# The values of a hybrid block's last four attention heads: products of 512 columns in place of 256, each for two token blocks, with the weights loaded once for each half of the tokens

## The chip, the cores and the metric

The kernel runs on one core of one Trainium2 chip. The metric is device time in microseconds (us) of one execution. The core has TensorE (PE, matrix products, with its weight loads PEld), VectorE (DVE), ScalarE (ACT), GpSimd (POOL) and SyncE (SP), whose queue issues nearly all transfers between the chip's main memory and the core. Engines run side by side, each through its own queue in order, and wait for one another by semaphores.

## The reference, cut to what matters

One layer: `x += W_out concat[StickBreakingAttn(6 heads), GatedConv(4 groups), GatedDeltaNet(6 heads)](RMSNorm(x))`, then a squared-ReLU MLP and a final norm; 512 tokens, model width 2048, all in float32. The part at hand is the stick-breaking attention, whose heads are 128 wide:

```python
proj = h @ w_in                      # sb_q, sb_k, sb_v are 768 columns each
z = einsum(q_blk, k) * scale
log_fail = where(causal, -softplus(z), 0.0)
rem = cumsum(log_fail, reverse=True) - log_fail
w = where(causal, exp(log_sigmoid(z) + rem), 0.0)
out = einsum(w, v)
```

The change concerns the columns of `sb_v` that belong to heads 2 to 5.

## The kernel before, in words

Every float32 operand of a large product is split into a high part in TensorE's fast float format and a low remainder; a product is three TensorE products: high by high, high by low, low by high (`mm3`, or the three lines in `v_stage`). The normalised input is kept in on-chip memory as 16 tiles `xw[k]` (128 rows of the model width by 512 tokens, high and low). Weights come through `wload`: a transfer of 128 x 512 numbers (256 KB) into `raw`, a cast on ScalarE into `whi` (L103), and a subtraction on VectorE into `wlo` (L104); each of the three has four buffers, and the function has a raised priority. `gemm` makes one 128 x 512 result in a PSUM bank `mm` (three banks) with four loads and 48 products of 512 columns, 12 to a load.

The kernel has these stages: a first pass over the input, which also makes the values of heads 0 and 1; the delta-net heads with the convolution groups; from about 525 us the stick-breaking heads; from about 740 us the output product (16 `gemm` results, one for each 128 of the model's columns); the MLP's two products.

A stick-breaking head `h` takes two `gemm` results, q and k (`sb_qk`, split by `sb_split` at L575, L576 and copied in part at L578), and the values (`vt[h // 2]`: high and low in `vhl`, the last block in full in `v3`). `sb_attn` is a chain: the products z (three lines of `mm3`, and a small one at L600) into three PSUM banks; scaling into `zs` (L601) and a mask on GpSimd (L604); L606 on VectorE; two steps on ScalarE (L607, L608); L610 and L611 on VectorE; four scans (L615); L617; an exponential on ScalarE (L618); ten transposes on TensorE (L626) into the same three banks; the split into `hl` (L630, L631, L633); ten products with the values into `o` (L639 to L643); and a copy into the head's `y` (L645). The tiles `zs`, `e`, `sp` and `hl` exist once, so one head's chain follows the other's.

The values of heads 2 and 3 are made by `v_stage(1)`, those of 4 and 5 by `v_stage(2)`: eight loads each, one load holding two row tiles of 256 columns, and for each row tile and each of the four token blocks three products of 256 columns, into halves of two `mm` banks. They are then scaled and split by `v_evac` (L230, L231, L234).

The order of instructions on each engine is not written out by hand. A scheduler places them when the kernel is built, by the program's order, priorities and its own estimate of durations; each engine then follows its list. The program's order in this stage before is: q and k of head 0, head 0, q and k of 1, head 1, `v_stage(1)`, q and k of 2, head 2, q and k of 3, head 3, q and k of 4, `v_stage(2)`, head 4, q and k of 5, head 5, and `gdn_gate(5)` (one `gemm`). Then follow the split of the 16 `y` tiles (L726, L727) and the output products; each of these runs through the `y` tiles in the order of `ORDER`, where head 5's is the 15th and head 5 of the delta net's the last.

Of the kernel before, what the change touches and what calls it, by code (L numbers as in the profile page):

```python
# [11 lines left out]
F32 = mybir.dt.float32  # L12
F32R = mybir.dt.float32r
AF = mybir.ActivationFunctionType
ALU = mybir.AluOpType

P = 128
T = 512
NB = T // P
D = 2048  # L20
KT = D // P
# [33 lines left out]
def trunk(ctx, tc, xT, wv1, wv2, wa, wo, wu, wd, vec, wf, out, dbg=None):  # L55
    nc = tc.nc
    V, S, G, PE = nc.vector, nc.scalar, nc.gpsimd, nc.tensor
# [39 lines left out]
    def wload(src, n, prio=None):  # L97
        with tc.high_priority(WPRIO if prio is None else prio):
            raw = per.tile([P, 512], F32, name="raw", tag="raw", bufs=4)
            nc.sync.dma_start(out=raw[:, :n], in_=src)  # L100
            hi = per.tile([P, 512], F32R, name="whi", tag="whi", bufs=4, align_bytes=256)
            lo = per.tile([P, 512], F32R, name="wlo", tag="wlo", bufs=4, align_bytes=256)
            S.copy(out=hi[:, :n], in_=raw[:, :n])  # L103
            V.tensor_tensor(out=lo[:, :n], in0=raw[:, :n], in1=hi[:, :n].bitcast(F32), op=ALU.subtract)  # L104
        return hi, lo
# [73 lines left out]
    xw = []  # L179
# [7 lines left out]
    for k in range(KT):  # L187
        hi, lo = wload(wv1[:, k, :], 268, 0)
# [6 lines left out]
                               op0=ALU.mult, op1=ALU.subtract)  # L195
        for b in range(NB):
            s = slice(b * P, (b + 1) * P)
# [15 lines left out]
    p = xps("r")  # L213
    PE.matmul(p, lhsT=ones, rhs=acc, start=True, stop=True)
    rsqrt_exp(R, p, 1.0 / D, None)
    rtok = pt([P, NB], "rtok")
    p = xps("r")
# [3 lines left out]
    rtoks = pt([P, NB], "rtoks")  # L221
    S.mul(out=rtoks, in_=rtok, mul=SCALE)

    def v_evac(src_of_blk, pool):

        hl = pool.tile([P, 2, NB, 256], F32R, name="vhl", bufs=2)
        v3 = pool.tile([P, 256], F32, name="v3", bufs=2)
        for b in range(NB):
            src = src_of_blk(b)
            S.activation(out=hl[:, 0, b], in_=src, func=AF.Copy, scale=rtok[:, b:b + 1])  # L230
            V.scalar_tensor_tensor(out=hl[:, 1, b], in0=src, scalar=rtok[:, b:b + 1],  # L231
                                   in1=hl[:, 0, b].bitcast(F32), op0=ALU.mult, op1=ALU.subtract)
            if b == NB - 1:
                S.activation(out=v3, in_=src, func=AF.Copy, scale=rtok[:, b:b + 1])  # L234
        return hl, v3

    vt = [None] * 3
    ab = pt([P, NB, 12], "ab")
# [8 lines left out]
        nc.sync.dma_start(out=vd[:, 2 * c:2 * c + 2].rearrange("p b f -> p (b f)"), in_=t)  # L247

    def v_load():
        hl = sp_pool.tile([P, 2, NB, 256], F32R, name="vhl", bufs=2)  # L250
        v3 = sp_pool.tile([P, 256], F32, name="v3", bufs=2)
        for c in range(2):
            t = tmp()
            nc.sync.dma_start(out=t, in_=vd[:, 2 * c:2 * c + 2].rearrange("p b f -> p (b f)"))
            o = hl[:, :, 2 * c:2 * c + 2].rearrange("p w b f -> p w (b f)")
            S.copy(out=o[:, 0], in_=t)
            V.tensor_tensor(out=o[:, 1], in0=t, in1=o[:, 0].bitcast(F32), op=ALU.subtract)
            if c == 1:
                S.copy(out=v3, in_=t[:, 256:512])
        vt[0] = (hl, v3)  # L260

    def v_stage(i):
        pp = [mmps(), mmps()]
        for c in range(0, KT, 2):
            hi, lo = wload(wv2[i - 1][:, c:c + 2, :].rearrange("p k f -> p (k f)"), 512)
            for kk in range(2):
                k = c + kk
                ws = slice(kk * 256, kk * 256 + 256)
                for b in range(NB):
                    s = slice(b * P, (b + 1) * P)  # L270
                    o = pp[b // 2][:, (b % 2) * 256:(b % 2) * 256 + 256]
                    PE.matmul(o, lhsT=xw[k][:, 0, s], rhs=hi[:, ws], start=k == 0 and b % 2 == 0, stop=False)  # L272
                    PE.matmul(o, lhsT=xw[k][:, 0, s], rhs=lo[:, ws], start=False, stop=False)  # L273
                    PE.matmul(o, lhsT=xw[k][:, 1, s], rhs=hi[:, ws], start=False, stop=k == KT - 1 and b % 2 == 1)  # L274
        vt[i] = v_evac(lambda b: pp[b // 2][:, (b % 2) * 256:(b % 2) * 256 + 256], sp_pool)

    ys = [None] * KT

# [294 lines left out]
    def sb_split(p, name):  # L573
        hl = sp_pool.tile([P, 2, 512], F32R, name=name, tag=name, bufs=2)
        S.copy(out=hl[:, 0], in_=p)  # L575
        V.tensor_tensor(out=hl[:, 1], in0=p, in1=hl[:, 0].bitcast(F32), op=ALU.subtract)  # L576
        l0 = sp_pool.tile([P, P], F32, name=name + "0", tag=name + "0", bufs=2)
        S.copy(out=l0, in_=p[:, 0:P])  # L578
        return hl, l0

# [2 lines left out]
    def sb_qk(h):  # L583
        qk[h] = sb_split(gemm(wa[24 + 2 * h], xw), "sq") + sb_split(gemm(wa[24 + 2 * h + 1], xw), "sk")
# [107 lines left out]
    v_load()  # L692
    sb_attn(0)
    sb_qk(1)
    sb_attn(1)
    v_stage(1)
    sb_qk(2)
    sb_attn(2)
    sb_qk(3)
    sb_attn(3)  # L700
    sb_qk(4)
    v_stage(2)
    sb_attn(4)
    sb_qk(5)
    sb_attn(5)
# [426 lines left out]
def layout(x, norm1_w, w_in, sc_conv_w, gdn_conv_w, gdn_a_log, gdn_dt_bias, gdn_norm_w,  # L1132
           w_out, norm2_w, w_up, w_down, final_norm_w):
    win = w_in[0]
    kc = lambda a: np.ascontiguousarray(a)
    cols = []
    for h in range(NH):
        cols += [3840 + 768 + h * P, 3840 + h * P, 3840 + 1536 + h * P]
    cols += [6144 + h * P for h in range(NH)]
    for h in range(NH):  # L1140
        cols += [h * P, 768 + h * P]
    for g in range(NG):
        cols += [2816 + g * P, 3328 + g * P, 2304 + g * P]
    wt = _ktile(win)
    wa = kc(np.stack([wt[:, :, c:c + P] for c in cols]))
    wv1 = kc(np.concatenate([wt[:, :, 1536:1792], wt[:, :, 6912:6924]], axis=2))
    wv2 = kc(np.stack([wt[:, :, 1792:2048], wt[:, :, 2048:2304]]))
    wo = _ktile(w_out[0]).reshape(P, KT, KT, P)[:, ORDER]
    wo = kc(wo.transpose(2, 0, 1, 3))


    wu = _ktile(w_up[0]).reshape(P, KT // 2, 2, FF // P // 2, 2, P)
    wu = kc(wu.transpose(3, 2, 4, 0, 1, 5).reshape(FF // P // 2, 2, 2, P, KT // 2 * P))


    wd = _ktile(w_down[0]).reshape(P, FF // P // (2 * HK), HK, 2, 2, 2, 512)
    wd = kc(wd.transpose(1, 5, 3, 4, 0, 2, 6).reshape(FF // P // (2 * HK), 2, 2, 2, P, HK * 512))
    wf = kc(np.broadcast_to(final_norm_w[None, :], (P, D)))
    pcol = lambda v: v.reshape(-1, P).T
    rep = lambda v: np.broadcast_to(v[None, :], (P, v.shape[0]))  # L1160
    scw = sc_conv_w[0].reshape(3, NG, P).transpose(2, 1, 0).reshape(P, 12)
    gcw = gdn_conv_w[0].reshape(4, 18, P).transpose(2, 1, 0).reshape(P, 72)
    vec = kc(np.concatenate([
        pcol(norm1_w[0]), pcol(norm2_w[0]), scw, gcw,
        rep(gdn_a_log[0]), rep(gdn_dt_bias[0]), gdn_norm_w[0].reshape(P, 1)], axis=1))
    xT = kc(_ktile(x[0].T))
    return dict(xT=xT, wv1=wv1, wv2=wv2, wa=wa, wo=wo, wu=wu, wd=wd, vec=vec, wf=wf)
# [14 lines left out]
```

## Time and profile before

| what | value |
|---|---|
| median of 3 runs | 2176.17 us (2174.32 to 2177.16) |
| the profiled execution, its own time | 2174.82 us |
| its span, first to last instruction | 2173.1 us |
| TensorE busy | 2143.5 us, 99% |
| VectorE, ScalarE, GpSimd busy | 77%, 49%, 6% |
| stick-breaking stage | about 525 to 740 us |

The span is what the views of the trace divide up; 1.7 us of the execution's own time lie around it. An engine's busy time counts an instruction from its start to its end; since TensorE's products overlap in a pipeline, the distance between their starts, not their duration, says how many fit into a time.

### The profile page before, as it was taken

Reading aid. Unit: us, or ns where it says so; the run is one execution under the profiler, and the core shown is the slowest. Engines: PE = TensorE matmul, PEld = TensorE weight load, DVE = VectorE, ACT = ScalarE, POOL = GpSimd, SP = SyncE. Lnnn points to the kernel's source line nnn. Section 1 sums busy time; section 2 is a strip of 40 time slices with the busy share of each in tenths; the row PEclk is TensorE's granted clock in tenths of the full one; section 3 lists DMA queues with packets and bytes.
Section 4 is the critical chain, followed back from the end, with each engine's and each line's share of the span. In section 5 each row is a group of like instructions: output and inputs, shape, how many; then the busy total and the mean of one; then the engine's idle time right before and its main releaser. Section 6 shows DMA issues by size and latency. Waiting matters only on the chain.

```text
span 2173.1 us, 33090 instructions
## 1 busy us (share of the span) xinstructions
PE 2143.5 (99%) x12674; PEld 1885.9 (87%) x12674; DVE 1663.8 (77%) x2348; ACT 1070.9 (49%) x1622; POOL 140.0 (6%) x191
## 2 busy tenths in 40 slices
PE   9999999999999999999999999999999999999997
PEld 8887888888988888799999999999788888888886
DVE  6688977644667655688788878887898898899887
ACT  5646665333435544454545444544444454445454
POOL 0000000000000011000000000000001010000102
PEclk9999999999999999999999999999999999999998
DMA  5333232322222344666666666656987777787764
GB/s 188 103 103 96 80 89 91 92 95 83 83 83 83 112 155 141 218 180 172 201 195 179 171 202 196 178 172 201 310 263 185 232 223 219 192 236 212 185 196 116
DMA packets 158974, 353.80 MB, mean 163 GB/s; under 512 B 20192, under 2 KB 61152, under 8 KB 158688
## 3 DMA queue, kind: packets, MB, share of 16 engines
q1 hardware_dynamic: 144704, 300.83, 40.9%
q0 software_dynamic: 13824, 50.34, 13.6%
q8 instruction: 99, 1.62, 0.3%
q14 instruction: 59, 0.48, 0.1%
q10 hardware_dynamic: 288, 0.52, 0.1%
HBM read 307.33 MB, written 44.31 MB: 162 GB/s over the span
## 4 chain that ended last, share of the span: by engine, by line
PE 94%; DMA 2%; DVE 2%; ACT 1%; issue 1%; SPq 0%; ACTq 0%; DVEq 0%
PE mm L110 11%; PE mm L109 11%; PE mm L111 11%; PE pu L109 10%; PE pu L111 10%; PE pu L110 10%; PE pp L110 9%; PE pp L109 9%; PE pp L111 9%; PE mm L273 1%; PE mm L274 1%; PE mm L272 1%; DMA xq<-xs 1%; DMA tmp<-x 1%; PE i L397 1%
## 5 line engine op out<-in xcount | busy, mean ns | idle before, releaser
L828 ACT CAST W<-q 128x1024 fp32r<-128x1024 f32 x446 | 465.4, 1051 | 573.7 <-PE pp L111 260.1
L829 DVE TENSOR_TENSOR W<-q,W 128x1024 fp32r<-128x1024 f32 x446 | 542.1, 1223 | 128.8 <-ACT W L828 124.5
L109 PE MATMUL mm<-big,whi 128*128 128x512 f32 x1024 | 404.6, 395 | 1.4 <-ACT whi L103 0.8
L110 PE MATMUL mm<-big,whi 128*128 128x512 f32 x1024 | 403.8, 394 | 0.0
L111 PE MATMUL mm<-big,wlo 128*128 128x512 f32 x1024 | 402.4, 393 | 0.0
L109 PE MATMUL pp<-W,A 128*128 128x512 f32 x896 | 348.3, 391 | 7.9 <-DVE xq L993 5.3
L110 PE MATMUL pp<-W,A 128*128 128x512 f32 x896 | 350.3, 391 | 2.1 <-DVE W L829 2.1
L111 PE MATMUL pp<-W,A 128*128 128x512 f32 x896 | 349.7, 390 | 1.1 <-DVE A L829 1.1
L104 DVE TENSOR_TENSOR wlo<-raw,whi 128x512 fp32r<-128x512 f32 (+1 forms) x292 | 196.3, 674 | 158.5 <-ACT whi L103 150.6
L103 ACT CAST whi<-raw 128x512 fp32r<-128x512 f32 (+1 forms) x292 | 176.9, 607 | 276.7 <-PE mm L110 238.7
L109 PE MATMUL pu<-XS,W 128*128 128x256 f32 x1024 | 288.4, 282 | 1.1 <-ACT W L828 0.6
L111 PE MATMUL pu<-XS,W 128*128 128x256 f32 x1024 | 287.7, 281 | 0.8 <-DVE W L829 0.8
L110 PE MATMUL pu<-XS,W 128*128 128x256 f32 x1024 | 288.0, 281 | 0.0
L109 PEld LDWEIGHTS mm<-big,whi 128*128 128x128 f32 x1024 | 192.4, 188 | 40.9 <-ACT whi L103 1.2
L110 PEld LDWEIGHTS mm<-big,whi 128*128 128x128 f32 x1024 | 192.5, 188 | 39.1 <-DVE big L727 0.3
L111 PEld LDWEIGHTS mm<-big,wlo 128*128 128x128 f32 x1024 | 192.4, 188 | 38.8
L109 PEld LDWEIGHTS pp<-W,A 128*128 128x128 f32 x896 | 169.1, 189 | 45.1 <-DVE xq L993 5.7
L110 PEld LDWEIGHTS pp<-W,A 128*128 128x128 f32 x896 | 169.1, 189 | 38.3 <-DVE W L829 3.3
L111 PEld LDWEIGHTS pp<-W,A 128*128 128x128 f32 x896 | 168.9, 189 | 36.6 <-DVE A L829 1.5
L846 DVE TENSOR_TENSOR q<-q 128x1024 f32<-128x1024 f32 x160 | 195.8, 1224 | 2.3 <-DMA q<-in_wu_dram 0.9
L109 PEld LDWEIGHTS pu<-XS,W 128*128 128x128 f32 x1024 | 194.1, 190 | 2.3 <-ACT W L828 1.5
L111 PEld LDWEIGHTS pu<-XS,W 128*128 128x128 f32 x1024 | 194.0, 190 | 1.0 <-DVE W L829 1.0
(290 smaller groups left out, 3269.1 us busy)
## 6 DMA issues: line engine op xcount, KB each, us to landing
q<-in_wu_dram SPq DMA_DIRECT2D x128, 512.0 KB, 4.5
q<-in_wd_dram SPq DMA_DIRECT2D x128, 512.0 KB, 5.5
raw<-in_wa_dram SPq DMA_DIRECT2D x192, 256.0 KB, 2.9
hs<-h SPq DMA_DIRECT2D x32, 1024.0 KB, 5.6
q<-in_wd_dram POOLq DMA_DIRECT2D x64, 512.0 KB, 7.5
ha<-hs SPq DMA_DIRECT2D x55, 512.0 KB, 6.4
raw<-in_wo_dram SPq DMA_DIRECT2D x64, 256.0 KB, 2.9
q<-in_wu_dram POOLq DMA_DIRECT2D x32, 512.0 KB, 5.5
```

What stands on the lines that cost most here:

```text
L103: S.copy(out=hi[:, :n], in_=raw[:, :n])
L104: V.tensor_tensor(out=lo[:, :n], in0=raw[:, :n], in1=hi[:, :n].bitcast(F32), op=ALU.subtract)
L109: PE.matmul(p, lhsT=lh, rhs=rh, start=first, stop=False, skip_group_check=more)
L110: PE.matmul(p, lhsT=lh, rhs=rl, start=False, stop=False, skip_group_check=more)
L111: PE.matmul(p, lhsT=ll, rhs=rh, start=False, stop=last, skip_group_check=more)
L272: PE.matmul(o, lhsT=xw[k][:, 0, s], rhs=hi[:, ws], start=k == 0 and b % 2 == 0, stop=False)
L273: PE.matmul(o, lhsT=xw[k][:, 0, s], rhs=lo[:, ws], start=False, stop=False)
L274: PE.matmul(o, lhsT=xw[k][:, 1, s], rhs=hi[:, ws], start=False, stop=k == KT - 1 and b % 2 == 1)
L397: PE.matmul(pv[:, b], lhsT=kq[:, 2 * c + b, 0], rhs=kq[:, 2 * c + b], start=True, stop=True)
L828: S.copy(out=o[:, 0], in_=src)
L829: V.tensor_tensor(out=o[:, 1], in0=src, in1=o[:, 0].bitcast(F32), op=ALU.subtract)
L846: on_v = lambda t, u: V.tensor_tensor(out=t, in0=t, in1=u, op=ALU.add)
```

## The change

`v_stage` goes, and `v_half` comes. Each load now holds one row tile of all 512 columns (heads 2 to 5), and `v_half(0)` multiplies it with token blocks 0 and 1, `v_half(1)` with blocks 2 and 3; the four heads' values of half the tokens come out of 16 loads and 96 products of 512 columns. The program has `v_half(0)` ahead of head 1 and `v_half(1)` ahead of head 2, since each half is needed from head 2 on. A third buffer for `vhl` holds all values at once, and the small copies `sq0` and `sk0` lose one of their two buffers. The weights' layout in memory is changed to match. Lines behind the edit move up by three to five: L626 becomes L623, L639 to L643 become L636 to L640, L100 to L111 stay.

```diff
--- before.py
+++ after.py
@@ -221,18 +221,13 @@
     rtoks = pt([P, NB], "rtoks")
     S.mul(out=rtoks, in_=rtok, mul=SCALE)
 
-    def v_evac(src_of_blk, pool):
-
-        hl = pool.tile([P, 2, NB, 256], F32R, name="vhl", bufs=2)
-        v3 = pool.tile([P, 256], F32, name="v3", bufs=2)
-        for b in range(NB):
-            src = src_of_blk(b)
-            S.activation(out=hl[:, 0, b], in_=src, func=AF.Copy, scale=rtok[:, b:b + 1])
-            V.scalar_tensor_tensor(out=hl[:, 1, b], in0=src, scalar=rtok[:, b:b + 1],
-                                   in1=hl[:, 0, b].bitcast(F32), op0=ALU.mult, op1=ALU.subtract)
-            if b == NB - 1:
-                S.activation(out=v3, in_=src, func=AF.Copy, scale=rtok[:, b:b + 1])
-        return hl, v3
+    def v_block(b, src, hl, v3):
+
+        S.activation(out=hl[:, 0, b], in_=src, func=AF.Copy, scale=rtok[:, b:b + 1])
+        V.scalar_tensor_tensor(out=hl[:, 1, b], in0=src, scalar=rtok[:, b:b + 1],
+                               in1=hl[:, 0, b].bitcast(F32), op0=ALU.mult, op1=ALU.subtract)
+        if b == NB - 1:
+            S.activation(out=v3, in_=src, func=AF.Copy, scale=rtok[:, b:b + 1])
 
     vt = [None] * 3
     ab = pt([P, NB, 12], "ab")
@@ -247,7 +242,7 @@
         nc.sync.dma_start(out=vd[:, 2 * c:2 * c + 2].rearrange("p b f -> p (b f)"), in_=t)
 
     def v_load():
-        hl = sp_pool.tile([P, 2, NB, 256], F32R, name="vhl", bufs=2)
+        hl = sp_pool.tile([P, 2, NB, 256], F32R, name="vhl", bufs=3)
         v3 = sp_pool.tile([P, 256], F32, name="v3", bufs=2)
         for c in range(2):
             t = tmp()
@@ -259,20 +254,22 @@
                 S.copy(out=v3, in_=t[:, 256:512])
         vt[0] = (hl, v3)
 
-    def v_stage(i):
+    def v_half(half):
+
         pp = [mmps(), mmps()]
-        for c in range(0, KT, 2):
-            hi, lo = wload(wv2[i - 1][:, c:c + 2, :].rearrange("p k f -> p (k f)"), 512)
-            for kk in range(2):
-                k = c + kk
-                ws = slice(kk * 256, kk * 256 + 256)
-                for b in range(NB):
-                    s = slice(b * P, (b + 1) * P)
-                    o = pp[b // 2][:, (b % 2) * 256:(b % 2) * 256 + 256]
-                    PE.matmul(o, lhsT=xw[k][:, 0, s], rhs=hi[:, ws], start=k == 0 and b % 2 == 0, stop=False)
-                    PE.matmul(o, lhsT=xw[k][:, 0, s], rhs=lo[:, ws], start=False, stop=False)
-                    PE.matmul(o, lhsT=xw[k][:, 1, s], rhs=hi[:, ws], start=False, stop=k == KT - 1 and b % 2 == 1)
-        vt[i] = v_evac(lambda b: pp[b // 2][:, (b % 2) * 256:(b % 2) * 256 + 256], sp_pool)
+        for k in range(KT):
+            hi, lo = wload(wv2[:, k], 512)
+            for i in range(2):
+                b = 2 * half + i
+                s = slice(b * P, (b + 1) * P)
+                mm3(pp[i], xw[k][:, 0, s], xw[k][:, 1, s], hi, lo, k == 0, k == KT - 1)
+        for i in range(2):
+            if half == 0:
+                vt[1 + i] = (sp_pool.tile([P, 2, NB, 256], F32R, name="vhl", bufs=3), None)
+            else:
+                vt[1 + i] = (vt[1 + i][0], sp_pool.tile([P, 256], F32, name="v3", bufs=2))
+            for j in range(2):
+                v_block(2 * half + j, pp[j][:, i * 256:i * 256 + 256], *vt[1 + i])
 
     ys = [None] * KT
 
@@ -574,7 +571,7 @@
         hl = sp_pool.tile([P, 2, 512], F32R, name=name, tag=name, bufs=2)
         S.copy(out=hl[:, 0], in_=p)
         V.tensor_tensor(out=hl[:, 1], in0=p, in1=hl[:, 0].bitcast(F32), op=ALU.subtract)
-        l0 = sp_pool.tile([P, P], F32, name=name + "0", tag=name + "0", bufs=2)
+        l0 = sp_pool.tile([P, P], F32, name=name + "0", tag=name + "0", bufs=1)
         S.copy(out=l0, in_=p[:, 0:P])
         return hl, l0
 
@@ -692,14 +689,14 @@
     v_load()
     sb_attn(0)
     sb_qk(1)
+    v_half(0)
     sb_attn(1)
-    v_stage(1)
     sb_qk(2)
+    v_half(1)
     sb_attn(2)
     sb_qk(3)
     sb_attn(3)
     sb_qk(4)
-    v_stage(2)
     sb_attn(4)
     sb_qk(5)
     sb_attn(5)
@@ -1144,7 +1141,7 @@
     wt = _ktile(win)
     wa = kc(np.stack([wt[:, :, c:c + P] for c in cols]))
     wv1 = kc(np.concatenate([wt[:, :, 1536:1792], wt[:, :, 6912:6924]], axis=2))
-    wv2 = kc(np.stack([wt[:, :, 1792:2048], wt[:, :, 2048:2304]]))
+    wv2 = kc(wt[:, :, 1792:2304])
     wo = _ktile(w_out[0]).reshape(P, KT, KT, P)[:, ORDER]
     wo = kc(wo.transpose(2, 0, 1, 3))
```

SP's queue, from the end of the delta-net stage to the first output weights; `raw` of `in_wv_dram` is a value load, of `in_wa_dram` one for `gemm`, of `in_wo_dram` one for the output product. Before:

```order
L254 DMA tmp<-vd 128x512 x2
L100 DMA raw<-in_wa_dram 128x512 x16
L100 DMA raw<-in_wv_dram 128x512 x8
L100 DMA raw<-in_wa_dram 128x512 x24
L100 DMA raw<-in_wv_dram 128x512 x8
L100 DMA raw<-in_wa_dram 128x512 x12
L100 DMA raw<-in_wo_dram 128x512 x17
```

and with the change:

```order
L249 DMA tmp<-vd 128x512 x2
L100 DMA raw<-in_wa_dram 128x512 x16
L100 DMA raw<-in_wv_dram 128x512 x16
L100 DMA raw<-in_wa_dram 128x512 x8
L100 DMA raw<-in_wv_dram 128x512 x16
L100 DMA raw<-in_wa_dram 128x512 x28
L100 DMA raw<-in_wo_dram 128x512 x17
```

The value loads are 32 in place of 16; 28 loads of q, k and gate weights stand behind the last of them, where 12 stood.

TensorE around head 5's transposes (`z<-ident,zs`); `o` is the product with the values, `mm<-big` here the output product. Before:

```order
L111 MATMUL mm<-big,wlo 128x512
L626 MATMUL z<-ident,zs 128x128 x10
L109 MATMUL mm<-big,whi 128x512
L110 MATMUL mm<-big,whi 128x512
L111 MATMUL mm<-big,wlo 128x512
...
L110 MATMUL mm<-big,whi 128x512
L639 MATMUL o<-hl,vhl 128x512
L111 MATMUL mm<-big,wlo 128x512
L109 MATMUL mm<-big,whi 128x512
...
L640 MATMUL o<-hl,vhl 128x512
L641 MATMUL o<-hl,vhl 128x512
```

and with the change, from the last product ahead of the transposes to the first behind the head:

```order
L111 MATMUL mm<-big,wlo 128x512
L623 MATMUL z<-ident,zs 128x128 x10
L636 MATMUL o<-hl,vhl 128x512
L637 MATMUL o<-hl,vhl 128x512
L638 MATMUL o<-hl,vhl 128x512
L636 MATMUL o<-hl,vhl 128x384
...
L638 MATMUL o<-hl,vhl 128x256
L640 MATMUL o<-w_6941,v_6189 128x128
L109 MATMUL mm<-big,whi 128x512 x3
L110 MATMUL mm<-big,whi 128x512
```

Output products stood between the transposes and the products `o`, and between the first and the second of these; now the ten follow the transposes directly. Ahead of the transposes, back to head 5's last z product, stand 81 products of 512 columns before, and 54 now.

VectorE in head 5's chain, from the step on the masked `zs` (L606 before, L603 now) to the split of the transposed weights (`hl`). Before:

```order
L606 SCALAR_TENSOR_TENSOR e<-zs 128x1280
L135 TENSOR_TENSOR tmp<-tmp 128x512
L104 TENSOR_TENSOR wlo<-raw,whi 128x512
L548 TENSOR_TENSOR y<-y,tmp 128x512
L610 SCALAR_TENSOR_TENSOR sp<-zs,e 128x1280
L104 TENSOR_TENSOR wlo<-raw,whi 128x512
L611 SCALAR_TENSOR_TENSOR zs<-zs,e 128x1280
L104 TENSOR_TENSOR wlo<-raw,whi 128x512
...
L615 SCALAR_TENSOR_TENSOR e<-ones,sp 128x255
L617 TENSOR_TENSOR zs<-zs,e 128x1280
L104 TENSOR_TENSOR wlo<-raw,whi 128x512 x3
L631 TENSOR_TENSOR hl<-z,hl 128x512 x2
```

and with the change:

```order
L603 SCALAR_TENSOR_TENSOR e<-zs 128x1280
L607 SCALAR_TENSOR_TENSOR sp<-zs,e 128x1280
L104 TENSOR_TENSOR wlo<-raw,whi 128x512
L608 SCALAR_TENSOR_TENSOR zs<-zs,e 128x1280
L104 TENSOR_TENSOR wlo<-raw,whi 128x512
...
L612 SCALAR_TENSOR_TENSOR e<-ones,sp 128x255
L104 TENSOR_TENSOR wlo<-raw,whi 128x512
L614 TENSOR_TENSOR zs<-zs,e 128x1280
L628 TENSOR_TENSOR hl<-z,hl 128x512 x2
L628 TENSOR_TENSOR hl<-z,hl 128x256
```

The gate's two steps (on `tmp` and `y`) stand ahead of it now, and the chain's own steps are the same ones.

## Rows read from the trace of the kernel before

**Rows 1.** The page: its head, TensorE's busy time (part 1), the chain (part 4).

```profile
span 2173.1 us, 33090 instructions
...
PE 2143.5 (99%) x12674; PEld 1885.9 (87%) x12674; DVE 1663.8 (77%) x2348; ACT 1070.9 (49%) x1622; POOL 140.0 (6%) x191
...
PE 94%; DMA 2%; DVE 2%; ACT 1%; issue 1%; SPq 0%; ACTq 0%; DVEq 0%
```

**Rows 2.** Windows, 525 to 740 us: length, then each engine's busy us (instructions).

```profile
525.00:740.00 215.00, 214.24 (x1191) 187.33 (x1190) 138.18 (x195) 99.11 (x171) 8.91 (x24) 1.00 0.26 81
```

**Rows 3.** Timeline of TensorE, 563 to 585 us: start, us, engine, line, operation.

```profile
564.02 0.28 PE L274 MATMUL mm<-whi,big 128*128 128x256 f32 x1
...
568.70 0.28 PE L274 MATMUL mm<-whi,big 128*128 128x256 f32 x1
...
569.98 0.39 PE L111 MATMUL mm<-big,wlo 128*128 128x512 f32 x1
...
584.94 0.39 PE L111 MATMUL mm<-big,wlo 128*128 128x512 f32 x1
```

**Rows 4.** Lines by shape, TensorE, 525 to 740 us: busy us, mean ns.

```profile
L273 PE MATMUL mm<-wlo,big 128*128 128x256 f32 x128 | 36.4, 285 | 0.0
```

**Rows 5.** Lines and DMA issues, 525 to 740 us: the loads' work.

```profile
L104 DVE TENSOR_TENSOR wlo<-raw,whi 128x512 fp32r<-128x512 f32 x65 | 44.7, 688 | 44.5 <-ACT whi L103 42.2 <-PE z L626 1.8
...
L103 ACT CAST whi<-raw 128x512 fp32r<-128x512 f32 x66 | 40.8, 619 | 69.6 <-PE mm L110 48.2 <-PE mm L274 17.0 <-issue 3.3
...
raw<-in_wv_dram SPq DMA_DIRECT2D x14, 256.0 KB, 2.7
```

**Rows 6.** Timeline of TensorE, 711 to 739 us, around head 5's steps.

```profile
712.19 0.39 PE L600 MATMUL z<-sk,sq 128*128 128x128 f32 x2
...
730.79 1.25 PE L626 MATMUL z<-ident,zs 128*128 128x128 f32 x10
...
731.80 0.48 PE L109 MATMUL mm<-big,whi 128*128 128x512 f32 x1
...
738.53 0.39 PE L643 MATMUL o<-w,v 128*128 128x128 f32 x2
```

**Rows 7.** Timeline of VectorE, 712 to 734 us, head 5's chain.

```profile
712.74 0.35 DVE L601 SCALAR_TENSOR_TENSOR zs<-z,rtoks,R 128x128 f32<-128x128 f32 x1
...
718.02 1.49 DVE L610 SCALAR_TENSOR_TENSOR sp<-zs,e 128x1280 f32<-128x1280 f32 x1 [0.85 <-ACT e L608]
...
719.42 0.68 DVE L104 TENSOR_TENSOR wlo<-raw,whi 128x512 fp32r<-128x512 f32 x1
...
722.50 2.96 DVE L615 TENSOR_TENSOR_SCAN e<-ones,sp 128x511 f32<-128x511 f32 x4
...
725.49 1.49 DVE L617 TENSOR_TENSOR zs<-zs,e 128x1280 f32<-128x1280 f32 x1
...
732.05 1.62 DVE L631 TENSOR_TENSOR hl<-z,hl 128x512 fp32r<-128x512 f32 x3
```

**Rows 8.** Timeline of ScalarE, 715 to 741 us, head 5's chain.

```profile
715.40 1.28 ACT L607 ACTIVATE e<-e 128x1280 f32<-128x1280 f32 x1 [0.34 <-DVE e L606]
...
727.08 1.27 ACT L618 ACTIVATE zs<-zs 128x1280 f32<-128x1280 f32 x1 [2.50 <-DVE zs L617]
...
738.95 0.59 ACT L645 COPY y<-o 128x512 f32<-128x512 f32 x1 [3.68 <-PE o L643]
...
739.95 1.14 ACT L726 CAST big<-y 128x512 fp32r<-128x512 f32 x2
```

**Rows 9.** Timeline: two waits; windows after the second, PEclk third from right.

```profile
1559.10 0.50 PE L110 MATMUL pp<-W,A 128*128 128x512 f32 x1 [1.41 <-DVE W L829]
...
1566.69 0.50 PE L109 MATMUL pp<-W,A 128*128 128x512 f32 x1 [2.08 <-ACT A L828]
...
1567.20:1570.40 3.20, 3.13 (x8) 2.19 (x8) 2.94 (x3) 1.43 (x2) 0.00 (x0) 0.50 1.03 251
...
1570.60:1573.80 3.20, 3.20 (x15) 2.63 (x15) 0.85 (x2) 1.05 (x1) 0.00 (x0) 1.00 1.08 398
```

## Prediction

> **What bounds the kernel now.** I read the page first. TensorE is busy in 99% of the span and the chain that ended last is 94% TensorE [rows 1], so what shortens or delays TensorE's own stream is what counts. The change lies in the stick-breaking stage, so the second view is the window 525 to 740 us, where TensorE is busy for 214.24 of 215 us, VectorE for 138.18 and ScalarE for 99.11, at a granted clock of 1.00 [rows 2]. TensorE has no wait there to be taken away. Two things can move the time: the length of its stream, and waits that do not exist yet. Busy time says nothing on length, since products overlap; I take start-to-start times from the timeline.
>
> **The products.** Before, v_stage runs 384 products of 256 columns (128 on each of three lines, [rows 4]). From 564.02 to 568.70 there are 39 steps between starts: 4.68/39 = 0.120 us each. Products of 512 columns: 569.98 to 584.94 in 66 steps, 14.96/66 = 0.2267 us [rows 3]. So 384 x 0.120 = 46.1 us become 192 x 0.2267 = 43.5 us, a gain of **2.5 us**. It is the fixed part of 192 products: 0.120 x 2 - 0.2267 = 0.0133 us each.
>
> On this fixed part the Trainium skill (TensorE: Matmul & The Clock Gate, section Back-to-back issue gap) gives a product's spacing as its columns at full rate plus about 2.5 ns. By it the gain would be only 192 x 0.0025 = 0.5 us, and the sum below 2.0 us worse. The rows disagree with it: their fixed part is five times that, so I keep 2.5 us.
>
> **The loads.** Each half loads all 16 row tiles, so 32 loads of 256 KB stand where 16 stood, landing in 2.7 us [rows 5]. The 16 new ones add 16 x 0.619 = 9.9 us of ScalarE casts and 16 x 0.688 = 11.0 us of VectorE subtractions [rows 5]. TensorE spends 6 x 0.2267 = 1.36 us on a load's products, where it spent 24 x 0.120 = 2.88. One buffer's round is landing 2.7, cast 0.62, subtraction 0.69 and some 0.5 of handing over (estimated from the 0.1 us steps between engines and the queue): 4.5 us; four buffers give a load in 1.13 us, under the 1.36. The room is small. In the first half head 0's steps share VectorE: four steps at 1.41 apart (718.02 to 719.42 shows the distance), scans 2.96, a k split 0.6 and eleven subtractions at 0.6 make 15.8 us against 68 x 0.2267 = 15.4 us of products ahead of head 0's transposes; up to four prepared loads (5.4 us) are ahead at the start. I put the starving at **0**. Bounds: nothing below it, since no wait is there to give back; above, one run of scans (2.96, [rows 7]) per half, 5.9 us. The nearest row is the 525 to 740 window, with no starving, but at half the load rate; hence the wide upper end. SP's queue carries these loads alone in this stage; what is behind them are the q and k weights, 16 loads later, with their buffers' lead.
>
> The copies at L578 with one buffer wait for the previous head's small product (L600); it is done before the exponential queued behind that copy can start, so nothing. The third vhl buffer is space alone. The results' evictions are the same 8 + 8 steps, only earlier, and no bank is asked for before they end: nothing.
>
> **What the move uncovers.** This is the term that decides. Each head is a serial chain: products z, VectorE and ScalarE steps, transposes, split, products o; one set of buffers (zs, e, sp) serves all heads, so they follow each other, and TensorE fills the chain's time with other products. Before, v_stage(2) stood between heads 3 and 4, so enough was left for head 5: 81 products between its last z product and its transposes (81 x 0.2267 = 18.4 us), and 14 to 22 more between transposes and o. Afterwards the v products are all used up by head 2. The later heads take the q and k products, the last gate and the output products ahead of time. The three mm banks allow the first three output products, and each needs head 5's y as its 15th of 16 row tiles. By the order, head 4's wait takes most of them, and exactly 54 products are left between head 5's last z product and its transposes; between transposes and o there is none. Nothing else independent exists there.
>
> How long the chain is, head 5 of before shows: last z product at 712.19 [rows 6], L601 712.74, ScalarE's L607 715.40, L610 718.02, scans 722.50, L617 725.49 to 726.98, L618 727.08 plus 1.27 = 728.35 [rows 7, 8]. That is 16.2 us. The order puts the same steps with four subtractions among them, and a cast for the fourth output product in front of the exponential on ScalarE; its buffer is free after 48 of the 54 products, 10.9 us in, so it delays nothing. TensorE has 0.15 for the small z product, 54 x 0.2267 = 12.24 and 0.1 for the switch: 12.5. Wait: 16.2 - 12.5 = **3.7 us**.
>
> From the transposes on: start 730.79, last split 732.05 + 1.62 = 733.67, 2.9 later [rows 6, 7]. The last three o products follow it (two at 0.12 behind it, then the small pair), so the pair starts at 3.15; y's copy came 0.42 after the pair (738.53 to 738.95) and takes 0.59, then the cast of the first big takes about 0.62 (half of 1.14 and its overlap, [rows 8]): 3.15 + 0.42 + 0.59 + 0.62 + 0.05 = 4.85 us to the next product. TensorE's work in it: transposes 730.79 to 731.80, 1.0 us [rows 6], and ten o products, 3 x 0.227 + 3 x 0.175 + 3 x 0.12 + 0.14 = 1.7: 2.7. Wait: **2.1 us**.
>
> For the earlier heads the same count leaves room: 92, 89, 95, 88 and 111 products, 19.9 us at least, against 16 to 18, and head 4, whose chain takes twelve splits of y in between (7 us on VectorE), has 25.2 us. So nothing.
>
> **The clock.** TensorE's wait at 1566.69 (2.08 us) was followed by a stretch at clock 0.50 (1.2 GHz in place of 2.4), 1567.2 to 1570.4, in which 8 products ran where 15 do at 1.00; a wait of 1.41 us left it at 1.00 [rows 9]. Waits of 3.7 and 2.1 us within 9 us should bring one such stretch: 7 x 0.227 = **1.6 us**. Bounds: none (0), or two stretches (3.2).
>
> **Sum**: - 2.5 + 0 + 3.7 + 2.1 + 1.6 = + 4.9 us. The profiled execution took 2174.8 us (span 2173.1), so it would give 2179.7. The median of the runs is 1.3 above that execution; on it the forecast is 2176.2 + 4.9 = **2181.1 us**, 0.23% slower. A measurement of this kernel tells apart about 0.2%, 4.35 us, so the bound is at 2180.5.
>
> **Rivals.** (1) The waits come and the clock stays at 1.00: + 3.3, 2179.5, no measurable change. For it: the wait can be cut in two by casts that hold products back, and 1.41 us did no harm; against it: 2.08 us did. (2) The halves starve as well. One run of scans ahead of a subtraction empties the buffers in one half: + 2.96 on the forecast, 2184.1. For it: 4.5 us for a round against 5.4 for four loads; against it: the lead and the alternation of the order. (3) Not slower: the chain runs at its floor. Its steps alone take 0.35 + 0.37 + 4 x 1.41 + 2.55 + 2.96 + 1.27 = 13.1 us without a step between or hand-over; TensorE would wait 0.6, and, if the o part loses half its wait, 1.0: - 2.5 + 1.6 = - 0.9, 2175.3. It decides only if chain and products differ by under 1 us. Against it: head 5 of before took 16.2 with the same steps. (4) The skill's spacing, told above, makes the forecast 2183.1 by a gain of 0.5 us; as a mechanism of this kernel it would be 512-column products that follow at 0.2373 rather than 0.2267. Against it stand 66 steps, so I give it no more than the upper part of the range.
>
> **How the numbers follow.** Forecast 0.50; clock stays 0.20; starving 0.17; floor 0.10; spacing 0.03. The likeliest gives 2181.1. Around it the waits' own uncertainty is about 1.5 us, and runs of one kernel differ by 2.8 us (2174.3 to 2177.2). The range leaves out the floor and the double ends of starving with clock: 2177.5 to 2186.0. Slower by over 0.2%: two thirds of the forecast (0.33), nearly all of starving and spacing (0.18), a fifth of rival 1 (0.04): 0.55. Faster by over 0.2% would need 4.4 us, more than the products give: 0.04, for what I overlook. Within: 0.41.
>
> **What would show it.** In the profile of after: the 512-column v products 0.227 apart; no TensorE wait on a subtraction inside the two halves; TensorE waiting about 3.7 us on the exponential (L618 of before) ahead of head 5's transposes and about 2 us more until the first output product with y; a clock below 1.00 there. If the stage's end moves earlier, or TensorE's idle time sits in the halves, the prediction is wrong; so too if head 5's chain takes clearly under 15 or over 18 us.

## The result, and the profile after

| | time |
|---|---|
| before, 20 runs beside it | 2175.72 us (2173.45 to 2178.31) |
| with the change, 20 runs | 2180.35 us (2177.99 to 2182.64) |
| ratio | 1.0020, 95% interval 1.0013 to 1.0027 |
| the profiled execution after, its own time | 2179.43 us, span 2177.7 us |

The changed kernel is 4.6 us slower by the medians (forecast 4.9), right at the bound of 0.2% that was named. The page of after, its head, the busy times and the chain:

```profile
span 2177.7 us, 32798 instructions
...
PE 2142.2 (98%) x12482; PEld 1876.4 (86%) x12482; DVE 1674.4 (77%) x2364; ACT 1080.5 (50%) x1638; POOL 140.8 (6%) x191
...
PE 93%; DMA 2%; DVE 2%; ACT 2%; issue 1%; SPq 0%; ACTq 0%; DVEq 0%
```

Against [rows 1]: 192 TensorE instructions fewer, VectorE 10.6 us and ScalarE 9.6 us busier, as the 16 new loads ask. TensorE's busy time hardly differs (2142.2 for 2143.5), while the rest of the span, in which it does nothing, grew from 29.6 to 35.5 us. The waits and the timeline of TensorE show where. First the waits of TensorE from 525 to 735 us (both halves and heads 0 to 4), then from 735 to 747 us:

```profile
PE z L109 <- ACT sk L572: 0.4, 1, 0.4
PE mm L109 <- ACT sq L575: 0.4, 1, 0.4
```

```profile
PE z L623 <- ACT zs L615: 3.4, 1, 3.4
PE mm L109 <- ACT big L723: 1.3, 1, 1.3
```

The timeline of TensorE after, around head 5 (start, duration, line, operation, idle time and its releaser), which answers [rows 6]:

```profile
723.44 0.39 PE L597 MATMUL z<-sk,sq 128*128 128x128 f32 x2
...
735.68 0.39 PE L111 MATMUL mm<-big,wlo 128*128 128x512 f32 x1
739.51 2.39 PE L623 MATMUL z<-ident,zs 128*128 128x128 f32 x10 [3.44 <-ACT zs L615]
741.56 0.78 PE L636 MATMUL o<-hl,vhl 128*128 128x512 f32 x1
...
743.72 0.39 PE L640 MATMUL o<-w,v 128*128 128x128 f32 x2
745.43 0.97 PE L109 MATMUL mm<-big,whi 128*128 128x512 f32 x3 [1.32 <-ACT big L723]
...
749.73 0.66 PE L764 MATMUL t<-ident,x 128*128 128x128 f32 x4
```

Before, the ten transposes started at 730.79 right behind a product [rows 6]. Now the last product starts at 735.68, the exponential (L615) is done at 739.46, and nothing stands between. The windows (length, busy us and instructions of PE, PEld, DVE, ACT, POOL, then the granted clock, third from right) answer [rows 2]:

```profile
525.00:745.00 220.00, 214.91 (x1004) 179.34 (x1002) 149.69 (x213) 108.20 (x187) 10.34 (x24) 0.99 0.32 101
...
739.40:742.60 3.20, 3.09 (x12) 2.81 (x13) 1.16 (x2) 1.50 (x4) 0.00 (x0) 0.50 0.06 23
742.60:746.00 3.40, 2.08 (x13) 1.71 (x11) 1.15 (x3) 1.99 (x4) 0.00 (x0) 1.00 0.00 0
```

TensorE was busy for all but 0.76 of 215 us before; here 5.1 of 220 are idle, and after the long wait the clock stands at 0.50 (1.2 in place of 2.4 GHz) for transposes and the first products with the values.

**The stage by two marks.** The first z product and the first transposes `t` of the output stage enclose what the change touches. Before, on TensorE:

```profile
527.38 0.67 PE L109 MATMUL z<-sk,sq 128*128 128x512 f32 x2 [0.35 <-ACT sk L575]
...
745.01 0.66 PE L767 MATMUL t<-ident,x 128*128 128x128 f32 x4
```

and after, where the second mark is the row at 749.73 above:

```profile
527.92 0.67 PE L109 MATMUL z<-sk,sq 128*128 128x512 f32 x2 [0.35 <-ACT sk L572]
```

217.63 us became 221.81: the stage is **4.2 us** longer. The 0.54 us ahead of it is none of the change's: TensorE's 2720 instructions there are the same ones in the same order, and the mark moves as much where nothing at all was changed ahead of it (527.33 in the second experiment, 528.09 in the last).

Head 5's last z product (712.19 before [rows 6], 723.44 after) cuts this stage in two. Ahead of it lie the halves and the other heads, behind it head 5's end. The products from the first mark up to it, counted by shape, before (L109 and L111 have as many as L110; the 384 products of 256 columns, 128 on each of L272 to L274 [rows 4], all lie in it):

```profile
L110 PE MATMUL mm<-big,whi 128*128 128x512 f32 x165 | 64.5, 391 | 0.0
```

and after (L109 and L111 have as many as L110):

```profile
L110 PE MATMUL mm<-big,whi 128*128 128x512 f32 x184 | 71.9, 391 | 0.0
L110 PE MATMUL mm<-wlo,big 128*128 128x512 f32 x64 | 25.1, 392 | 0.0
```

With the heads' own products, the same 169 in both, 495 products of 512 columns and 384 of 256 took 184.81 us before; 744 of 512 columns took 195.52 after. The 744 are the 495, the 192 of the two halves, and 57 more that the new order brings forward, which are 57 x 0.2267 = 12.9 us. The stretch grew by only 10.7, so the new products, with whatever they have to wait for, take **2.2 us less** than the old ones. Head 5's end became 6.4 us longer: 32.82 us with 129 such products before, 26.29 with 72 after. These stretches repeat well: up to head 5's last z product 184.82 us in the last experiment, which has the old products, and 195.49 to 195.55 in the second, fourth and fifth, which have the new.

### The profile page after: what moved, and what is told of

Its sections match the earlier page's. It is cut to its first block, busy times and chain, and to the rows that moved or that the text cites. A ratio compares the mean times of both kernels' runs of the same rounds, so it can differ in the third digit from the quotient of the medians.

```text
span 2177.7 us, 32798 instructions
## 1 busy us (share of the span) xinstructions
PE 2142.2 (98%) x12482; PEld 1876.4 (86%) x12482; DVE 1674.4 (77%) x2364; ACT 1080.5 (50%) x1638; POOL 140.8 (6%) x191
## 4 chain that ended last, share of the span: by engine, by line
PE 93%; DMA 2%; ACT 2%; DVE 2%; issue 1%; SPq 0%; ACTq 0%; DVEq 0%
PE mm L109 11%; PE mm L110 11%; PE mm L111 11%; PE pu L110 10%; PE pu L111 9%; PE pu L109 9%; PE pp L110 9%; PE pp L109 9%; PE pp L111 9%; DMA xq<-xs 1%; PE i L394 1%; DMA tmp<-x 1%; DVE W L826 1%; DMA q<-in_wd_dram 0%; PE z L623 0%
## 5 line engine op out<-in xcount | busy, mean ns | idle before, releaser
L109 PE MATMUL mm<-big,whi 128*128 128x512 f32 x1024 | 404.3, 395 | 3.3 <-ACT whi L103 1.4
L110 PE MATMUL mm<-big,whi 128*128 128x512 f32 x1024 | 403.5, 394 | 0.0
L111 PE MATMUL mm<-big,wlo 128*128 128x512 f32 x1024 | 401.9, 393 | 0.0
L109 PE MATMUL pp<-W,A 128*128 128x512 f32 x896 | 348.4, 391 | 7.9 <-DVE xq L990 5.3
L110 PE MATMUL pp<-W,A 128*128 128x512 f32 x896 | 350.6, 391 | 2.6 <-DVE W L826 2.6
L111 PE MATMUL pp<-W,A 128*128 128x512 f32 x896 | 350.2, 391 | 1.1 <-DVE A L826 1.1
L103 ACT CAST whi<-raw 128x512 fp32r<-128x512 f32 (+1 forms) x308 | 186.9, 608 | 287.1 <-PE mm L110 249.6
L104 DVE TENSOR_TENSOR wlo<-raw,whi 128x512 fp32r<-128x512 f32 (+1 forms) x308 | 207.0, 676 | 144.9 <-ACT whi L103 139.1
L109 PE MATMUL pu<-XS,W 128*128 128x256 f32 x1024 | 288.1, 281 | 1.8 <-ACT W L825 1.6
L111 PE MATMUL pu<-XS,W 128*128 128x256 f32 x1024 | 287.8, 281 | 0.8 <-DVE W L826 0.8
L110 PE MATMUL pu<-XS,W 128*128 128x256 f32 x1024 | 287.9, 281 | 0.0
L109 PEld LDWEIGHTS mm<-big,whi 128*128 128x128 f32 x1024 | 192.3, 188 | 42.6 <-ACT whi L103 1.9
L111 PEld LDWEIGHTS mm<-big,wlo 128*128 128x128 f32 x1024 | 192.4, 188 | 39.1
L110 PEld LDWEIGHTS mm<-big,whi 128*128 128x128 f32 x1024 | 192.4, 188 | 39.0 <-DVE big L724 0.2
L109 PEld LDWEIGHTS pp<-W,A 128*128 128x128 f32 x896 | 169.2, 189 | 45.0 <-DVE xq L990 5.7
L110 PEld LDWEIGHTS pp<-W,A 128*128 128x128 f32 x896 | 169.2, 189 | 38.8 <-DVE W L826 3.8
L111 PEld LDWEIGHTS pp<-W,A 128*128 128x128 f32 x896 | 169.2, 189 | 36.7 <-DVE A L826 1.8
L109 PEld LDWEIGHTS pu<-XS,W 128*128 128x128 f32 x1024 | 194.0, 189 | 2.8 <-ACT W L825 2.4
L111 PEld LDWEIGHTS pu<-XS,W 128*128 128x128 f32 x1024 | 194.0, 189 | 1.0 <-DVE W L826 1.0
```

The costliest lines, as they stand in the source:

```text
L109: PE.matmul(p, lhsT=lh, rhs=rh, start=first, stop=False, skip_group_check=more)
L110: PE.matmul(p, lhsT=lh, rhs=rl, start=False, stop=False, skip_group_check=more)
L111: PE.matmul(p, lhsT=ll, rhs=rh, start=False, stop=last, skip_group_check=more)
```

## The experiments

Two theories stood against each other. **Shortage**: the early values use up the independent products that TensorE ran during the later heads' chains, so head 5's chain lies bare; products and loads play no other part. **Stream**: the loss is in the halves themselves, through doubled loads or products that gain less than reckoned. The first two runs move the shortage alone, without and with the change.

**The move alone, without the new products.** The kernel before, with v_stage(1) ahead of head 1 and v_stage(2) ahead of head 2, and the buffers as in the change. Products and loads are those of before.

```diff
     sb_qk(1)
+    v_stage(1)
     sb_attn(1)
-    v_stage(1)
     sb_qk(2)
+    v_stage(2)
     sb_attn(2)
     sb_qk(3)
     sb_attn(3)
     sb_qk(4)
-    v_stage(2)
     sb_attn(4)
```

> The kernel before with its two value stages moved forward (ahead of head 1 and of head 2), still 256-column products and 16 loads, with the third vhl buffer and the single sq0 and sk0. Theory (the wait of head 5's chain is what costs): the order leaves 25 products of 512 columns between head 5's last z product and its transposes, 0.15 + 25 x 0.2267 + 0.09 = 5.9 us, against a chain of 16.2, so a wait of 10.3 us, then 2.1 us until the output products go on, and 1.4 to 3.2 us for the clock: slower than before by 13.8 to 15.6 us, no TensorE wait elsewhere in the stage. Rival (the double loads or the halves cost the time): neither is here, so the time of before, within 1 us.

2187.14 us (2186.26 to 2189.32), ratio 1.0051 (1.0038 to 1.0063): 10.9 us slower than the kernel before beside it (2176.24). Its TensorE around head 5, its VectorE (chain steps L610 to L615), and the window of low clock:

```profile
738.06 0.39 PE L111 MATMUL mm<-big,wlo 128*128 128x512 f32 x1
746.65 2.40 PE L626 MATMUL z<-ident,zs 128*128 128x128 f32 x10 [8.20 <-ACT zs L618]
```

```profile
734.97 0.68 DVE L104 TENSOR_TENSOR wlo<-raw,whi 128x512 fp32r<-128x512 f32 x1
737.70 1.49 DVE L610 SCALAR_TENSOR_TENSOR sp<-zs,e 128x1280 f32<-128x1280 f32 x1 [2.05 <-ACT e L608]
739.22 1.49 DVE L611 SCALAR_TENSOR_TENSOR zs<-zs,e 128x1280 f32<-128x1280 f32 x1
740.75 2.96 DVE L615 TENSOR_TENSOR_SCAN e<-ones,sp 128x511 f32<-128x511 f32 x4
```

```profile
740.70:750.90 10.20, 4.25 (x16) 3.86 (x17) 6.18 (x9) 2.98 (x5) 0.00 (x0) 0.50 0.00 0
```

The move alone does more harm than the whole change, in the place that the shortage names: 8.2 us on the exponential. The size was over-estimated: 13.8 to 15.6 us were expected, and by the two marks, 527.50 and 757.43 here, the stage is 12.3 us longer. The VectorE rows say why. I had taken the chain of [rows 7, 8], 16.2 us, with the weight subtractions that stand among its steps, three there and four in the changed kernel. With nothing left to multiply there is nothing left to prepare: one subtraction stands among them here, the other steps follow at 1.5 us, and the chain takes 14.2 (732.39, the start of the last z product, to 746.60, the exponential's end). Of the 1.8 us to the changed kernel's 16.0, 1.4 lie where a subtraction stands right between two steps there and none does here; no row names a cause for the 0.4 ahead of the first of these steps. So a shortage can shorten the chain that it lays bare.

**Head 5's y as the last row tile.** The changed kernel, with the last two entries of `ORDER` exchanged. Each of the three output products ahead of time can then run 45 of 48 products before it needs head 5, so 63 stand ahead of the transposes in place of 54.

```diff
-ORDER = [10, 11, 12, 6, 7, 8, 9, 0, 1, 2, 3, 13, 4, 14, 5, 15]
+ORDER = [10, 11, 12, 6, 7, 8, 9, 0, 1, 2, 3, 13, 4, 14, 15, 5]
```

> The changed kernel with head 5's y as the 16th row tile of the output products instead of the 15th (the last two of ORDER exchanged; the weights' layout follows). Theory: three more products for each of three banks, 63 instead of 54, so the wait ahead of head 5's transposes shrinks by 9 x 0.2267 = 2.0 us to 1.6; what follows the transposes stays 2.1. Time 2.0 us below the changed kernel, or 3.4 below if the shorter wait leaves the clock at 1.00. Rival (the time is lost in the two halves): no change against the changed kernel.

2176.74 us (2175.14 to 2178.45), ratio 1.0002 (0.9993 to 1.0011). Of the 4.6 us that the change cost, 0.5 are left. TensorE's waits from 735 to 746 us:

```profile
PE mm L109 <- ACT big L723: 1.3, 1, 1.3
PE z L623 <- ACT zs L615: 0.9, 1, 0.9
PE o L637 <- DVE hl L628: 0.2, 1, 0.2
```

3.4 became 0.9, though only 9 products (2.0 us) came in between. The other 0.5 us is the chain: from the last z product to the transposes it takes 15.6 us here (722.82 to 738.41) and 16.1 in after (723.44 to 739.51), because a subtraction that stands between L607 and L608 there stands elsewhere here. VectorE in after:

```profile
729.14 1.49 DVE L607 SCALAR_TENSOR_TENSOR sp<-zs,e 128x1280 f32<-128x1280 f32 x1 [2.65 <-ACT e L605]
730.55 0.69 DVE L104 TENSOR_TENSOR wlo<-raw,whi 128x512 fp32r<-128x512 f32 x1
731.15 1.49 DVE L608 SCALAR_TENSOR_TENSOR zs<-zs,e 128x1280 f32<-128x1280 f32 x1
```

and here:

```profile
728.52 1.49 DVE L607 SCALAR_TENSOR_TENSOR sp<-zs,e 128x1280 f32<-128x1280 f32 x1 [2.65 <-ACT e L605]
730.04 1.49 DVE L608 SCALAR_TENSOR_TENSOR zs<-zs,e 128x1280 f32<-128x1280 f32 x1
```

Over these waits the clock stayed up (window 737 to 746 us, 1.00 third from right):

```profile
737.00:746.00 9.00, 6.55 (x34) 4.56 (x33) 3.78 (x7) 5.20 (x10) 0.00 (x0) 1.00 0.22 78
```

So the end of the expectation that has the clock in it came true, and products and loads, which this kernel has as the change made them, cost nothing that can be seen: against the stream theory.

**The last gate's neighbour moved back.** To give head 5's chain 48 products more, gdn_gate(4), one gemm that stands ahead of the stage, goes behind gdn_gate(5).

```diff
-    gdn_gate(4)
...
     gdn_gate(5)
+    gdn_gate(4)
```

> The changed kernel with gate 4 of the delta net (48 products, 10.9 us) taken from the delta-net stage and put behind gate 5. The order then has 87 products ahead of head 5's transposes (19.7 us against a chain of 16.2) and 15 between these and the products o. Theory: both waits and the low clock go, 7.1 us below the changed kernel and 2.5 below before (what the wider products save). Rivals: the delta-net stage lacks the 48 products and waits in its last scan, up to 7 us given back there; or the saving of 2.5 us isn't real and the time is that of before.

2183.46 us (2181.66 to 2185.02), ratio 1.0034 (1.0022 to 1.0046): 7.2 us slower than before, the rival's side. Head 5's transposes no longer wait (first row), but the delta net's tail ahead of the stage does (the two longest waits from 440 to 530 us), and the clock fell there:

```profile
738.35 0.39 PE L110 MATMUL mm<-big,whi 128*128 128x512 f32 x1
738.58 1.25 PE L623 MATMUL z<-ident,zs 128*128 128x128 f32 x10
```

```profile
PE o L534 <- DVE MT L531: 3.7, 1, 3.7
PE z L109 <- ACT sk L572: 1.7, 1, 1.7
```

```profile
519.80:526.60 6.80, 4.70 (x15) 3.91 (x16) 4.40 (x8) 3.82 (x9) 0.27 (x1) 0.50 0.00 0
```

The kernel before waits for 0.4 us at two places in that window and nowhere else. The first z product, which the 48 products fewer should bring from 527.38 to 516.5 us, starts at 523.02: 6.5 us are given back there, near the 7 that the rival named. Behind head 5 the theory failed too, for after the products o nothing was left to multiply, and the wait on the copy of y stayed (waits from 736 to 750 us):

```profile
PE mm L109 <- ACT big L723: 1.3, 1, 1.3
```

The gate was cover too, for another chain. Cover moved from one place to another is a debt at the first.

**Work in the wait, for the clock alone.** The changed kernel, with three products of the identity and a tile that is at hand, between the last output product and the transposes; nobody reads their results.

```diff
+        if h == 5:
+            warm = xps("z")
+            for i in range(3):
+                PE.matmul(warm, lhsT=ident, rhs=e[:, 512 * (i % 2):512 * (i % 2) + 512], start=True, stop=True)
```

> The changed kernel with three unused float32 products of 512 columns (0.43 us for each of their two passes, 2.6 us in all), which read what the scans of head 5 leave and so run inside the wait ahead of its transposes. Theory (part of the loss is the clock that falls to 0.50 after the wait): the clock stays at 1.00, the ten transposes take 1.1 instead of 2.4 us, 1.3 us below the changed kernel. Rival (the clock costs nothing, since the chain alone sets the end): the time of the changed kernel.

2179.40 us (2177.89 to 2180.49), ratio 1.0013 (1.0004 to 1.0022). That is 1.5 us under the changed kernel by the ratios, each to the kernel before beside it, and 0.95 by the medians; the two intervals overlap, so the times alone don't settle it. TensorE and the window (clock 1.00 up to 742.6):

```profile
735.41 2.74 PE L618 MATMUL z<-e,ident 128*128 128x512 f32 x6
739.00 1.31 PE L627 MATMUL z<-ident,zs 128*128 128x128 f32 x10 [0.86 <-ACT zs L619]
...
744.23 0.97 PE L109 MATMUL mm<-big,whi 128*128 128x512 f32 x3 [1.33 <-ACT big L727]
```

```profile
735.50:742.60 7.10, 6.00 (x27) 3.55 (x26) 3.71 (x6) 2.89 (x5) 0.00 (x0) 1.00 0.25 74
```

Idle time before the transposes turned into useless work, which frees nothing: what was saved is the clock. From the transposes to the first output product it takes 744.23 - 739.00 = 5.23 us, in after 745.43 - 739.51 = 5.92. So the low clock cost **0.7 us** there, and the two marks (527.38 and 748.54 here, 221.16 us apart) give the same 0.7 for the stage. The expectation, 1.3, is too high by the trace.

**A fourth bank.** The second run's kernel, with one more accumulation bank, for the fourth output product; its first 12 products then stand behind head 5's products with the values.

```diff
-    def gemm(src, acts):
-        p = mmps()
+    def gemm(src, acts, p=None):
+        p = mmps() if p is None else p
...
-    psl = psum_pool("ps_l", t=2)
+    psl = psum_pool("ps_l", w=1, t=2)
...
+    w0 = xps("w")
...
-        p = gemm(wo[m], yh)
+        p = gemm(wo[m], yh, w0 if m == 3 else None)
```

(In what follows, "1.9990" is a slip for 0.9990.)

> The changed kernel with the exchange of the last two row tiles (as in the second run) and one more accumulation bank of its own for the fourth output product. By the order of the instructions the first 12 products of this one stand between head 5's ten products o and the first product that needs head 5's y. In the second run TensorE waited 1.53 us there. Theory (TensorE is short of products that don't depend on head 5): 12 x 0.2267 = 2.7 us of work cover the 1.53 us, so the time falls by 1.5 us against the second run, to 1.9990 to 1.0000 of the kernel before in ratio terms 0.999 to 1.000, about 2175.2 us; the wait of about 1 us ahead of the transposes stays. Rival (the load buffers are the limit: three of the four hold the last weights of the three products in flight): the weights of the fourth product are not there, TensorE waits for a subtraction on VectorE in place of the copy of y, and the time is that of the second run, 2176.7 us.

2175.05 us (2173.24 to 2176.73), ratio 0.9998 (0.9989 to 1.0007) to before (2175.56 beside it). TensorE behind head 5, and its waits from 736 to 746 us:

```profile
742.27 0.39 PE L640 MATMUL o<-w,v 128*128 128x128 f32 x2
742.41 0.48 PE L109 MATMUL w<-big,whi 128*128 128x512 f32 x1
```

```profile
PE z L623 <- ACT zs L615: 0.9, 1, 0.9
PE o L637 <- DVE hl L628: 0.2, 1, 0.2
```

The wait on the copy of y is gone; the weights were there. The step against the second run, 0.0004 in the ratio or about 0.9 us, goes the way of the 1.5 expected, but the two intervals overlap, so the trace shows the wait gone and the times don't show the gain. This version is faster than the changed kernel, and cannot be told from the kernel before.

**The exchange on the kernel before.** The control for the second run: 87 products stand ahead of head 5's transposes in place of 81.

```diff
-ORDER = [10, 11, 12, 6, 7, 8, 9, 0, 1, 2, 3, 13, 4, 14, 5, 15]
+ORDER = [10, 11, 12, 6, 7, 8, 9, 0, 1, 2, 3, 13, 4, 14, 15, 5]
```

> The kernel before with the same exchange alone: head 5's y as the last of the 16 row tiles of the output product, in place of the last but one. Theory: before, 81 products stood ahead of head 5's transposes and TensorE waited for nothing there, so six more products ahead of them (87 by the order) cover no wait, and the time is that of the kernel before, ratio 1.000 (0.9995 to 1.0005). What the exchange gave the changed kernel is then repayment of a shortage that the change itself made. Rival: the exchange is a gain of its own, about 3 us in either kernel (ratio 0.9985).

2174.55 us (2173.15 to 2178.00), ratio 0.9999 (0.9990 to 1.0008): no difference, and the rival's 0.9985 lies outside the interval. TensorE starts the transposes right behind a product:

```profile
732.64 0.39 PE L111 MATMUL mm<-big,wlo 128*128 128x512 f32 x1
732.87 1.25 PE L626 MATMUL z<-ident,zs 128*128 128x128 f32 x10
```

The exchange is worth some 4 us (from ratio 1.0020 to 1.0002) where products are short, and nothing where they are not. What it gave was repayment.

## Why the prediction was right, point by point

**The sum came near, by the mechanism that was named and with some luck.** Forecast + 4.9, measured + 4.6 by the medians and + 4.2 in the stage by its two marks. By the terms, with the waits taken from the starts of TensorE's rows, the one behind the transposes and the clock with the help of the fourth run, where the clock stayed up:

| term | predicted | in the traces |
|---|---|---|
| products | - 2.5 | - 2.2, with any starving in it |
| starving in the halves | 0 | no such wait |
| wait ahead of the transposes | + 3.7 | + 3.5 |
| wait from the transposes to the first product with y | + 2.1 | + 2.5 |
| clock | + 1.6 | + 0.7 |
| not accounted for | | - 0.3 |
| sum | + 4.9 | + 4.2 |

The misses, from 0.2 to 0.9 us, go both ways and partly cancel. So it is partly luck that the forecast came within 0.3 us of the medians; that it named the waits, their places and the fall of the clock is not.

**The products.** In the first half, on TensorE (L111 of each group of three):

```profile
559.62 0.39 PE L111 MATMUL mm<-whi,big 128*128 128x512 f32 x1
...
561.66 0.39 PE L111 MATMUL mm<-whi,big 128*128 128x512 f32 x1
```

2.04 us for 9 steps are 0.2267 each, the number of [rows 3]. The gain itself is the 2.2 us of the stretch up to head 5's last z product. Against the move alone, which has the old products in the new places, it comes to 2.8 (204.89 us with 581 products of 512 columns and 384 of 256); the 2.5 lies between. The Trainium skill (TensorE: Matmul & The Clock Gate, section Back-to-back issue gap) gives a spacing, which it calls that of an isolated product, by which the gain would be 0.5 us as an estimate; the 2.2 and 2.8 disagree with it, as [rows 3] did. Rival 4, products 0.2373 apart (0.2375 by its own terms), falls.

**The loads.** TensorE has no wait on a cast or a subtraction of weights from 525 to 735 us; its two waits of 0.4 us are on head 0's q and k, and before has them too. Rival 2 falls, and with it the stream theory: the halves, products and loads together, take 2.2 us less than the old value stages did. VectorE's and ScalarE's 10.6 and 9.6 us (reckoned: 11.0 and 9.9) lie wholly beside other work.

**The chain and its cover.** ScalarE after, the exponential of head 5 and the copies of y, which answers [rows 8]:

```profile
738.19 1.27 ACT L615 ACTIVATE zs<-zs 128x1280 f32<-128x1280 f32 x1 [3.04 <-DVE zs L614]
...
744.14 0.59 ACT L642 COPY y<-o 128x512 f32<-128x512 f32 x1 [1.02 <-PE o L640]
744.76 1.14 ACT L723 CAST big<-y 128x512 fp32r<-128x512 f32 x2
```

From the last z product (723.44) to the exponential's end (739.46) the chain took 16.0 us, for 16.2 reckoned; the last product's start (735.68), 0.23 for it and 0.1 for the switch leave 3.5 us to the transposes. Rival 3, the chain at its floor, falls with that. The move alone came closer to it, at 14.2, for want of subtractions: the 16.2 is right only as long as weights are still prepared, as the order showed for after, and I left that out of the experiment's expectation. That nothing else independent existed there held for the order, not for the work: the exchange found nine more products ahead of the transposes, the fourth bank twelve behind the products o.

**Behind the transposes.** At full clock the part takes 5.23 us (the fourth run), of which 2.7 are work: 2.5 of wait. I had reckoned 4.85 (the terms as written add up to 4.83) and 2.1. The steps from the last pair on are as forecast (743.72 to 744.14 is 0.42, the copy 0.59, the cast 0.6). What was too short is the way to that pair: 3.15 reckoned, 3.5 in the fourth run (739.00 to 742.52), where the second product o waits 0.2 more for its split.

**The clock** is the term that was mis-sized most. In the profiled execution it fell as forecast and for about as long (the window above); rival 1 falls. But the 1.6 took the whole low stretch as full of work, seven products lost. Here only the transposes and the first products o ran in it; the rest was waiting on ScalarE and VectorE, whose steps took no longer in it (the first split's cast, L627, 0.59 us and its subtraction, L628, 0.69; at 1.00 the copy L642 took 0.59 and a subtraction L104 0.69). The transposes took 2.05 us to the next start (739.51 to 741.56), 1.0 more than in [rows 6]; but with the clock up, in the fourth run, the first product o comes 1.33 us behind their start (739.00 to 740.33) and the second waits for its split, so that part of the 1.0 is time that would have been waited anyway: 0.7 net.

What remains open: the 0.3 us by which the terms, 6.7 at head 5's end, are over the 6.4 that the marks leave for it; and why the gain of the products is 0.6 us larger against the move alone than against before.

## What to carry to other kernels

Work that seems to be in no one's way may be what an engine does while a serial chain runs elsewhere; before it is moved or shortened, count how many independent instructions stand between the chain's start and its end, and what is left of them afterwards. Here 54 products for a chain of 16 us turned a gain of some 2.5 us into a loss of 4.6. Repay the shortage with work that needs the chain's result last (an order of sums, one more bank), not with work that covers another chain. Repaid, this kernel is back at the time of before, and not measurably faster.

## What the runs showed of the hardware that I had not expected

In a TensorE wait of 3.5 us the granted clock fell to 0.50, in one of 8.3 us too, and there it stayed for 10.2 us, over half of them idle; with waits of 0.9, 0.2 and 1.3 us within 6 it stayed at 1.00. Ten transposes took 2.05 us to the next start at 0.50 and 1.01 at 1.00 [rows 6]: the low clock doubles what runs, but its price is what of the stretch is work, 0.7 us here, not the stretch's share. Useless products in a wait kept the clock up. And the three products of full float32 in the fourth run stand in the trace as six records in 2.74 us, 592 ns each in the mean and 0.43 us from start to start, where a product of 512 columns in the fast format takes some 390 ns and follows after 0.2267 us.
